# Down-projection of a gated FFN: four activation tiles per PSUM bank instead of two, half of the columns at a time

## The chip, the cores and the metric

One core of a Trainium2 chip runs the whole kernel. TensorE (PE) does the matmuls, with its weight loads as a row of their own (PEld); VectorE (DVE), ScalarE (ACT) and GpSimd (POOL) do the rest; SyncE (SP) issues the transfers. The metric is the device time of the program in microseconds (us), the median over several runs.

## The reference, cut to what matters

One decoder block over 2048 tokens of width 1024, in float32. A state-space branch and a sparse attention branch (an indexer picks 256 keys for each query) are merged by gates and added to the residual `x`; a SwiGLU feed-forward network of width 2816 follows:

```python
x = x + merged @ w_out
h2 = rms(x, norm2_g)
x = x + (silu(h2 @ w_ffn_gate) * (h2 @ w_ffn_up)) @ w_ffn_down
```

The change concerns the last product, `... @ w_ffn_down`, of shape (2048, 2816) by (2816, 1024).

## The kernel before, in words

**Float32 in three products.** Each operand is split into a high and a low part of a reduced float32 format, and `mm3` adds three matmuls (high by high, high by low, low by high) into one PSUM bank of 128 x 512 values. So one 128-row slice of a contraction costs three matmuls.

**Three generators and a planner.** The program is written as generators: the state-space branch, the attention branch, and the dense part (merge, output projection, FFN). A planner, the class `Pace`, runs them when the program is built, not on the chip: it keeps for each engine the time at which it would be free, adds a cost of its own for each instruction, and each time lets that generator go on whose next step can start (attention is asked before the dense part). What comes out is one fixed order of instructions for each engine; on the chip every engine works through its own in that order. All instructions are recorded by one helper, so the trace puts all of them on line L206. The steps of the attention's search for the 256 best keys (`search`) are counting passes on VectorE (tile `jkd`) and ScalarE (`jka`); one on VectorE may be placed while VectorE is, by the plan, at most `AHEAD` = 7 us further than PE. The cost of such a pass in the plan (a `tensor_scalar` with an accumulated output over 2-byte values) is

```python
RATE = {"DVE": (1.05e-3, 0.07), ...}      # us per element, us each
cost = size * r + c
cost -= size * r / 2                      # all operands of 2 bytes
cost += 0.14                              # accum_out
```

**The dense part** works in four blocks of 512 tokens (`block`, `tb` = 0 to 3). A block computes the merge (tiles `act`, `mg`) and the output projection into the residual `x1` (tile `x` in the trace), normalizes and transposes it (tiles `h`), and then goes over the 22 slices `f` of the FFN's width. `up(f)` makes gate and up product of a slice (48 matmuls, tiles `ww` for weights and `f` for banks), and `gate` and `join` turn them into an activation tile `at` (high and low part, 128 x 512 each) on ScalarE and VectorE. After every second `up`, `down` multiplies the two activation tiles of the pair before with their two slices of `w_ffn_down` (tile `wd`): for four token tiles and two halves of the columns it sums 2 x 3 matmuls in a bank, and VectorE adds the bank to `x1`. The last pair is multiplied right after `up(21)`.

**Banks.** While the attention is not finished a block has three PSUM banks for this, and four more during the search; the last block has eight.

**Weights.** In block 0 each weight is loaded raw (512 KB), split into high and low by two instructions on any of three engines, and the pair is stored to DRAM (`wc`, 1 MB); later blocks load the pair from there. The class `Rings` keeps one list of items in the order of use; an item is only issued when all before it are. Tiles of the kind "w" have a ring of three. Tiles of the kind "d" hold two items each, and their ring holds one such tile (two in the last block): the next two items are issued or split after `drop("d")`, when the last matmul has read the tile. A block's last items stand ahead of the next block's first in the list. All transfers go through SP's queue in order. Between `up(21)` and the last `down`, SP also issues the loads of the next block's `act` tiles (`load_branch`, 4 MB).

Of the kernel before, what the change touches and what calls it, by code (L numbers as in the profile page):

```python
# [13 lines left out]
F32R = mybir.dt.float32r  # L14
# [20 lines left out]
NF = DFF // 128  # L35
# [16 lines left out]
class Pace:  # L52
# [95 lines left out]
    def at(self, eng, *what):  # L148

        return lambda: self.when(eng, what) + (None,)  # L150
# [215 lines left out]
class Block:  # L366
# [1257 lines left out]
    def weights(self):  # L1624

        a = self.a
        items = []
        for ct in range(KD):
            items.append(("w", lambda raw, ct=ct: [
                (raw[:, i * 512:(i + 1) * 512].rearrange("p (k c) -> p k c", k=4),  # L1630
                 a[w][0, :, ct * 128:(ct + 1) * 128].rearrange("(k p) c -> p k c", p=128))
                for i, w in enumerate(("w_proj_ssm", "w_proj_attn"))]))
        for cg in range(4):
            for b in range(2):
                items.append(("w", lambda raw, cg=cg, b=b: [
                    (raw.rearrange("p (k c) -> p k c", k=4),
                     a["w_out"][0, b * 512:(b + 1) * 512, cg * 256:(cg + 1) * 256]
                     .rearrange("(k p) c -> p k c", p=128))]))
        for f in range(NF):
            for w in ("w_ffn_gate", "w_ffn_up"):  # L1640
                items.append(("w", lambda raw, f=f, w=w: [
                    (raw.rearrange("p (k c) -> p k c", k=KD),
                     a[w][0, :, f * 128:(f + 1) * 128].rearrange("(k p) c -> p k c", p=128))]))

            n = f if f % 2 == 0 else f + 1 if f == NF - 1 else 0
            for q in range(max(n - 2, 0), n):
                items.append(("d", lambda raw, q=q: [(raw, a["w_ffn_down"][0, q * 128:(q + 1) * 128])]))
        copies = [self.dram.tile([128, 2, 1024], F32, name=f"wc{i}") for i in range(len(items))]
        return [(kind, parts, copy, tb > 0) for tb in range(NB) for (kind, parts), copy in zip(items, copies)]

    def load_branch(self, bigp, br, tb):

        z = bigp.tile([128, 2, 4, TB], F32R, name=f"act{br}")
        for k in range(4):
            self.nc.sync.dma_start(z[:, :, k].bitcast(F32), (self.act_d, self.att_d)[br][tb][:, :, k])
        return z

    def block(self, tb, bigp, ld, nps, nd):

        nc, a, at = self.nc, self.a, self.pace.at  # L1660
        n = TB
        t0 = tb * TB
        nt = n // 128
# [3 lines left out]
        with ExitStack() as st:  # L1667
# [25 lines left out]
            def ready(*w):  # L1693
                return at("PE", free, *w)

            with ExitStack() as sm:
                mp = self.pool(sm, "mg", 1)
                mg = mp.tile([128, 2, KD, n], F32R, name="mg")
                with ExitStack() as sp:
# [16 lines left out]
                    for q, (ct, br) in enumerate([(0, 0), (1, 0), (0, 1), (1, 1)] +  # L1716
                                                 [(ct, br) for ct in range(2, KD) for br in range(2)]):
                        w = ld.get("w", 1 if q == 1 else 0)
                        w = w.rearrange("p z a (b k c) -> p (z a) b k c", b=2, k=4)[:, :, br]
# [16 lines left out]
                        if q in (4, 6, 8, 10):  # L1736
                            t = q // 2 - 2
# [25 lines left out]
                for cg in range(D // NC):  # L1763
                    cl = slice(cg * NC, (cg + 1) * NC)
                    for t in range(0, nt, 2):
                        for k in range(KD):
                            if k % 2 == 0:

                                late = t == nt - 2 and k >= 4
                                w = ld.get("w", 0 if late or k < 4 else 1)  # L1770
                                w = w.rearrange("p z a (k c) -> p (z a) k c", k=4)
# [3 lines left out]
                            for j in range(2):  # L1775
                                tl = slice((t + j) * 128, (t + j + 1) * 128)
# [17 lines left out]
                def up0(g, between=()):  # L1794

                    first[g] = bank(False)
                    sl = slice(g * 256, (g + 1) * 256)
                    for i in range(2):
                        w = ld.get("w", i).rearrange("p z a (k c) -> p (z a) k c", k=KD)
                        for k in range(KD):  # L1800
                            if k % 4 == 0:
                                yield at("PE", w)
                            z = hT[k // 4]
                            self.mm3(first[g][:, i * 256:(i + 1) * 256], w[:, 0, k], w[:, 1, k], z[:, 0, k % 4, sl],
                                     z[:, 1, k % 4, sl], i == k == 0, i == 1 and k == KD - 1)
                            if k % 2 == 1:
                                ld.tick()
                        if i == 0:
                            for t in between:
                                yield ready(hs[t])  # L1810
                                turn(t)
# [8 lines left out]
                yield ready(*hT)  # L1820
                yield from up0(0, (2, 3))
                self.pace.tight = False
            ap = self.pool(st, "fa", 3)
            tp = self.pool(st, "ft", 2)
            ld.ring("d", self.pool(st, "fd", nd), nd, 2)

            def gate(p):

                t = tp.tile([128, p.shape[1]], F32, name="t", tag="t")
                if self.exps:  # L1830

                    nc.scalar.activation(t, p, AF.Tanh, scale=0.5)
                    nc.vector.scalar_tensor_tensor(t, t, 1.0, p, op0=ALU.add, op1=ALU.mult)
                    return t, 0.5
                nc.scalar.activation(t, p, AF.Silu)
                return t, 1.0

            def join(t, c, p, hi, lo):
                nc.vector.scalar_tensor_tensor(t, t, c, p, op0=ALU.mult, op1=ALU.mult)
                self.split(t, hi, lo, nc.scalar, nc.vector)  # L1840

            def up(f, acts):
                if f == 0:
                    yield ready(*hT)
                    yield from up0(1)
                    for _ in range(2):
                        ld.drop("w")
                    for g, p in enumerate(first):
                        sl = slice(g * 256, (g + 1) * 256)
                        t, c = gate(p[:, :256])  # L1850
                        join(t, c, p[:, 256:], acts[:, 0, sl], acts[:, 1, sl])
                    return
                for i in range(2):
                    w = ld.get("w").rearrange("p z a (k c) -> p (z a) k c", k=KD)
                    yield ready(w, *hT)
                    p = bank()
                    for k in range(KD):
                        z = hT[k // 4]
                        self.mm3(p, w[:, 0, k], w[:, 1, k], z[:, 0, k % 4], z[:, 1, k % 4], k == 0, k == KD - 1)
                        if k == KD - 1:  # L1860
                            ld.drop("w")
                        if k % 2 == 1:
                            ld.tick()
                            if k < KD - 1:
                                yield at("PE")
                    if i == 0:
                        t, c = gate(p)
                join(t, c, p, acts[:, 0], acts[:, 1])

            def out(t):  # L1870
                nc.sync.dma_start(self.out[0, t0 + t * 128:t0 + (t + 1) * 128], x1[:, t])

            def down(acts, last):
                w = ld.get("d")
                for t in range(nt):
                    tl = slice(t * 128, (t + 1) * 128)
                    for cg in range(2):
                        cl = slice(cg * 512, (cg + 1) * 512)
                        yield ready(w, *acts)
                        p = bank()  # L1880
                        for f in range(2):
                            self.mm3(p, acts[f][:, 0, tl], acts[f][:, 1, tl], w[:, 0, f, cl], w[:, 1, f, cl],
                                     f == 0, f == 1)
                        if t == nt - 1 and cg == 1:
                            ld.drop("d")
                        ld.tick()
                        nc.vector.tensor_tensor(x1[:, t, cl], p, x1[:, t, cl], op=ALU.add)
                    if last and t > 0:
                        out(t - 1)
                if last:  # L1890
                    out(nt - 1)

            prev = None
            for c in range(NF // 2):
                acts = []
                for f in (2 * c, 2 * c + 1):
                    acts.append(ap.tile([128, 2, n], F32R, name="at"))
                    yield from up(f, acts[-1])
                    if f % 2 == 0 and prev:
                        yield from down(prev, False)  # L1900
                prev = acts
            if tb + 1 < NB:
                self.act = [self.load_branch(bigp, br, tb + 1) for br in range(1 + (self.attended >= 4 * (tb + 2)))]
            yield from down(prev, True)
            more.close()
            self.lent = False
            del ld.pools["d"]
# [78 lines left out]
```

## Time and profile before

| | |
|---|---|
| median of 3 runs | 3467.05 us (3461.62 to 3470.55) |
| the profiled execution: its own time | 3462.75 us |
| its span, first to last instruction | 3460.6 us |
| mean granted TensorE clock | 0.965 |
| busy: PE / VectorE / ScalarE / GpSimd | 93% / 62% / 36% / 20% |

Read as stretches (us from the span's start): up to about 1044 projections, state-space branch and first attention tiles; block 0 from there to 1685, block 1 to 2342, block 2 to 2996, block 3 to the end. The search for the key tiles 8 to 11 lies in about 1392 to 1800, that for 12 to 15 in about 2088 to 2450; attention proper in 1827 to 2088 and 2523 to 2900.

### The profile page before, as it was taken

To read this page: it belongs to the slowest core of one execution; us is meant where nothing else is said; L and a number is where in the kernel's file an instruction comes from. 1 tells how busy PE (TensorE), PEld (TensorE's weight loads), DVE (VectorE), ACT (ScalarE), POOL (GpSimd) and SP (SyncE) were. 2 spreads that over 40 slices of the span, in tenths; PEclk is the share of its full clock that TensorE was granted. 3 is DMA by queue.
4 is the path that set the end of the run, shared out by engine and by line. 5 is a ranking of instruction groups with operands and counts; after the bars stand their busy time and mean duration, and the time that the engine had idled before them with its cause. 6 is when DMAs were issued, how large, how long until landed. Compare 5 with 4: busy or idle time off the path is not lost. (4 is left out here: it accounts for less than half of the span.)

```text
span 3460.6 us, 44348 instructions
## 1 busy us (share of the span) xinstructions
PE 3201.6 (93%) x16292; PEld 2698.5 (78%) x16292; DVE 2133.6 (62%) x4306; ACT 1261.8 (36%) x2187; POOL 706.1 (20%) x1003
## 2 busy tenths in 40 slices
PE   6999999898878999989889999988899999999999
PEld 5889777676756888767688888767788888798887
DVE  4565665656496666788776766996856664222222
ACT  3141444445542544465024444771233442010000
POOL 3333686852213122244100000001000000000000
PEclk8999999999988999999999999999999999999999
DMA  4834333433448566567755233556453324755544
GB/s 134 248 119 121 117 110 89 147 124 105 146 148 300 208 212 228 182 232 244 286 184 194 97 133 135 194 195 242 176 200 121 134 86 152 282 214 215 195 170 182
DMA packets 321529, 605.69 MB, mean 175 GB/s; under 512 B 52896, under 2 KB 205216, under 8 KB 290592
## 3 DMA queue, kind: packets, MB, share of 16 engines
q1 hardware_dynamic: 321312, 602.86, 49.9%
q8 instruction: 128, 2.10, 0.3%
q14 instruction: 89, 0.73, 0.1%
HBM read 434.71 MB, written 166.89 MB: 174 GB/s over the span
## 5 line engine op out<-in xcount | busy, mean ns | idle before, releaser
L206 PE MATMUL f<-h,ww 128*128 128x512 f32 (+1 forms) x4416 | 1012.8, 383 | 3.0 <-DVE h L206 1.4
L206 PEld LDWEIGHTS f<-h,ww 128*128 128x128 f32 x4416 | 800.6, 190 | 159.9 <-DVE h L206 2.2
L206 PE MATMUL f<-wd,at 128*128 128x512 f32 x2112 | 530.8, 403 | 60.4 <-ACT at L206 31.9
L206 PEld LDWEIGHTS f<-wd,at 128*128 128x128 f32 x2112 | 403.5, 194 | 156.3 <-ACT at L206 27.9
L206 PE MATMUL gps<-hT,gw 128*128 128x512 f32 x1536 | 390.5, 404 | 17.3 <-ACT gsg L206 14.7
L206 ACT ACTIVATE jka<-S,tr 128x1024 bf16<-128x1024 f32 (+6 forms) x217 | 305.6, 1408 | 172.4 <-DVE tr L206 127.0
L206 PEld LDWEIGHTS gps<-hT,gw 128*128 128x128 f32 x1536 | 287.9, 192 | 81.5 <-ACT gsg L206 17.3
L206 DVE TENSOR_TENSOR x<-f,x 128x512 f32<-128x512 f32 x352 | 237.2, 686 | 91.3 <-PE f L206 90.5
L206 PE MATMUL mm<-w,hT 128*128 128x512 f32 (+1 forms) x1152 | 282.2, 403 | 7.4 <-DVE hT L206 7.1
L206 DVE SCALAR_TENSOR_TENSOR t<-t,f 128x512 f32<-128x512 f32 (+1 forms) x124 | 82.3, 664 | 329.5 <-PE f L206 284.4
L206 PEld LDWEIGHTS mm<-w,hT 128*128 128x128 f32 x1152 | 242.3, 241 | 32.5 <-DVE hT L206 8.5
L206 DVE TENSOR_TENSOR tl<-pt,th 128x512 fp32r<-128x512 f32 (+1 forms) x288 | 183.9, 658 | 131.7 <-ACT th L206 130.4
L206 ACT CAST th<-pt 128x512 fp32r<-128x512 f32 (+1 forms) x288 | 156.0, 563 | 233.5 <-PE pt L206 231.5
L206 POOL TENSOR_TENSOR g<-g,g 128x512 f32<-128x512 f32 x32 | 42.1, 1317 | 915.9 <-issue 551.8
L206 PE MATMUL f<-act,ww 128*128 128x512 f32 x768 | 190.8, 410 | 29.2 <-DMA act<-act 9.0
L206 PE MATMUL f<-ww,mg 128*128 128x256 f32 x1536 | 197.6, 291 | 18.3 <-DMA ww<-wc 10.0
L206 PEld LDWEIGHTS f<-ww,mg 128*128 128x128 f32 x1536 | 193.8, 199 | 21.3 <-issue 8.5
L206 PEld LDWEIGHTS f<-act,ww 128*128 128x128 f32 x768 | 150.8, 199 | 69.0 <-issue 14.3
L206 ACT ACTIVATE P<-P,m 128x1024 f32<-128x1024 f32 (+7 forms) x192 | 172.1, 899 | 72.6 <-DVE m L206 72.0
L206 PE MATMUL lg<-kk,q 128*128 128x512 f32 (+1 forms) x640 | 184.1, 390 | 5.8 <-DMA kk<-kk 3.7
L206 ACT ACTIVATE t<-f 128x512 f32<-128x512 f32 (+1 forms) x92 | 53.0, 576 | 331.7 <-PE f L206 331.6
L206 ACT CAST at<-t 128x512 fp32r<-128x512 f32 (+1 forms) x92 | 55.2, 600 | 325.2 <-DVE t L206 325.1
(347 smaller groups left out, 4577.1 us busy)
## 6 DMA issues: line engine op xcount, KB each, us to landing
ww<-wc SPq DMA_DIRECT2D x180, 1024.0 KB, 5.0
wd<-wc SPq DMA_DIRECT2D x66, 1024.0 KB, 8.5
wc<-ww SPq DMA_DIRECT2D x60, 1024.0 KB, 7.8
raw<-in_w_in_dram SPq DMA_DIRECT2D x104, 256.0 KB, 3.3
wc<-wd SPq DMA_DIRECT2D x22, 1024.0 KB, 7.5
x<-in_x_dram SPq DMA_DIRECT2D x32, 512.0 KB, 5.2
gate<-gsg SPq DMA_DIRECT2D x64, 256.0 KB, 2.2
g<-gate SPq DMA_DIRECT2D x64, 256.0 KB, 5.3
```

The lines of the kernel that those rows point to most:

```text
L206: return f(*args, **kw)
```

## The change

Four activation tiles instead of two are summed in a bank, so that a bank takes 12 matmuls, and VectorE adds it to `x1` half as often. A call of `down` covers half of the columns (512) for four slices, in place of all columns for two; the items of `w_ffn_down` become 256 rows by 512 columns, still two to a tile. `due` says which quarter is multiplied after which `up`: slices q to q+3 have their first half after `up(q+4)` and their second after `up(q+6)`. Seven activation tiles are kept instead of three. Slices 0 to 19 make five groups of four; the second half of the fifth group and the pair 20, 21 (both halves, 6 matmuls to a bank) are multiplied after `up(21)`. The matmuls, their shapes and their number stay.

```diff
--- before.py
+++ after.py
@@ -1642,11 +1642,21 @@
                     (raw.rearrange("p (k c) -> p k c", k=KD),
                      a[w][0, :, f * 128:(f + 1) * 128].rearrange("(k p) c -> p k c", p=128))]))
 
-            n = f if f % 2 == 0 else f + 1 if f == NF - 1 else 0
-            for q in range(max(n - 2, 0), n):
-                items.append(("d", lambda raw, q=q: [(raw, a["w_ffn_down"][0, q * 128:(q + 1) * 128])]))
+            for q, cg in self.due(f):
+                for p in range(q, min(q + 4, NF), 2):
+                    items.append(("d", lambda raw, p=p, cg=cg: [
+                        (raw.rearrange("p (f c) -> p f c", f=2),
+                         a["w_ffn_down"][0, p * 128:(p + 2) * 128, cg * 512:(cg + 1) * 512]
+                         .rearrange("(f p) c -> p f c", p=128))]))
         copies = [self.dram.tile([128, 2, 1024], F32, name=f"wc{i}") for i in range(len(items))]
         return [(kind, parts, copy, tb > 0) for tb in range(NB) for (kind, parts), copy in zip(items, copies)]
+
+    def due(self, f):
+
+        full = NF // 4 * 4
+        if f == NF - 1:
+            return [(full - 4, 1)] + [(full, cg) for cg in range(2)]
+        return [(f - 4 - f % 4, f % 4 // 2)] if f >= 4 and f % 2 == 0 else []
 
     def load_branch(self, bigp, br, tb):
 
@@ -1820,7 +1830,7 @@
                 yield ready(*hT)
                 yield from up0(0, (2, 3))
                 self.pace.tight = False
-            ap = self.pool(st, "fa", 3)
+            ap = self.pool(st, "fa", 7)
             tp = self.pool(st, "ft", 2)
             ld.ring("d", self.pool(st, "fd", nd), nd, 2)
 
@@ -1870,38 +1880,43 @@
             def out(t):
                 nc.sync.dma_start(self.out[0, t0 + t * 128:t0 + (t + 1) * 128], x1[:, t])
 
-            def down(acts, last):
-                w = ld.get("d")
+            def down(q, cgs):
+
+                w = ld.get("d").rearrange("p z a (f c) -> p z (a f) c", f=2)
+                nf = min(4, NF - q)
                 for t in range(nt):
                     tl = slice(t * 128, (t + 1) * 128)
-                    for cg in range(2):
+                    for cg in cgs:
                         cl = slice(cg * 512, (cg + 1) * 512)
-                        yield ready(w, *acts)
+                        yield ready(w, *(acts[q + f] for f in range(nf)))
                         p = bank()
-                        for f in range(2):
-                            self.mm3(p, acts[f][:, 0, tl], acts[f][:, 1, tl], w[:, 0, f, cl], w[:, 1, f, cl],
-                                     f == 0, f == 1)
-                        if t == nt - 1 and cg == 1:
+                        for f in range(nf):
+                            z, o = acts[q + f], f + nf * (cg if len(cgs) > 1 else 0)
+                            self.mm3(p, z[:, 0, tl], z[:, 1, tl], w[:, 0, o, cl0], w[:, 1, o, cl0],
+                                     f == 0, f == nf - 1)
+                            if f % 2 == 1:
+                                ld.tick()
+                                if f < nf - 1:
+                                    yield at("PE")
+                        if t == nt - 1 and cg == cgs[-1]:
                             ld.drop("d")
-                        ld.tick()
                         nc.vector.tensor_tensor(x1[:, t, cl], p, x1[:, t, cl], op=ALU.add)
-                    if last and t > 0:
+                    if len(cgs) > 1 and t > 0:
                         out(t - 1)
-                if last:
+                if len(cgs) > 1:
                     out(nt - 1)
 
-            prev = None
-            for c in range(NF // 2):
-                acts = []
-                for f in (2 * c, 2 * c + 1):
-                    acts.append(ap.tile([128, 2, n], F32R, name="at"))
-                    yield from up(f, acts[-1])
-                    if f % 2 == 0 and prev:
-                        yield from down(prev, False)
-                prev = acts
+            acts, cl0 = {}, slice(0, 512)
+            for f in range(NF):
+                acts[f] = ap.tile([128, 2, n], F32R, name="at")
+                yield from up(f, acts[f])
+                if f < NF - 1:
+                    for q, cg in self.due(f):
+                        yield from down(q, (cg,))
             if tb + 1 < NB:
                 self.act = [self.load_branch(bigp, br, tb + 1) for br in range(1 + (self.attended >= 4 * (tb + 2)))]
-            yield from down(prev, True)
+            yield from down(NF // 4 * 4 - 4, (1,))
+            yield from down(NF // 4 * 4, (0, 1))
             more.close()
             self.lent = False
             del ld.pools["d"]
```

## Rows read from the trace of the kernel before

**Rows 1.** page, part 1 (busy time by engine) and part 2 (40 slices)

```profile
PE 3201.6 (93%) x16292; PEld 2698.5 (78%) x16292; DVE 2133.6 (62%) x4306; ACT 1261.8 (36%) x2187; POOL 706.1 (20%) x1003
...
PE   6999999898878999989889999988899999999999
```

**Rows 2.** page, part 5, costliest groups: busy us, mean ns | idle before, releaser

```profile
L206 PE MATMUL f<-wd,at 128*128 128x512 f32 x2112 | 530.8, 403 | 60.4 <-ACT at L206 31.9
...
L206 DVE TENSOR_TENSOR x<-f,x 128x512 f32<-128x512 f32 x352 | 237.2, 686 | 91.3 <-PE f L206 90.5
```

**Rows 3.** windows: stretch, its length, busy us (instructions) per engine, clock, DMA

```profile
1465.00:1655.00 190.00, 166.77 (x671) 133.04 (x670) 169.10 (x308) 105.86 (x137) 88.20 (x41) 0.93 0.69 236
1655.00:1690.00 35.00, 18.70 (x70) 14.46 (x69) 33.27 (x63) 0.62 (x1) 0.00 (x0) 0.76 0.64 248
...
2175.00:2315.00 140.00, 130.68 (x556) 105.46 (x555) 129.69 (x268) 108.39 (x114) 0.00 (x0) 0.98 0.46 176
2315.00:2342.00 27.00, 13.47 (x50) 10.19 (x48) 25.66 (x52) 14.48 (x16) 0.00 (x0) 0.76 0.70 249
...
2523.00:2983.00 460.00, 460.00 (x2501) 390.33 (x2500) 265.02 (x552) 164.80 (x305) 0.00 (x0) 1.00 0.38 143
```

**Rows 4.** windows of tile x alone, the additions to the residual: VectorE is third

```profile
1465.00:1655.00 190.00, 0.00 (x0) 0.00 (x0) 25.88 (x39) 0.00 (x0) 0.93 0.69 236
...
2175.00:2315.00 140.00, 0.00 (x0) 0.00 (x0) 20.67 (x32) 0.00 (x0) 0.98 0.46 176
```

**Rows 5.** waits of PE, 1465 to 1655: total, times, longest us

```profile
PE f L206 <- DVE wd L206: 9.4, 4, 2.6
PE f L206 <- DVE un L206: 6.9, 3, 3.5
```

**Rows 6.** timeline of PE, block 3: start, us, instructions [idle before, releaser]

```profile
3422.06 11.04 PE L206 MATMUL f<-wd,at 128*128 128x512 f32 x48
3432.94 11.04 PE L206 MATMUL f<-h,ww 128*128 128x512 f32 x48
...
3445.48 10.77 PE L206 MATMUL f<-wd,at 128*128 128x512 f32 x45 [0.82 <-ACT at L206]
```

**Rows 7.** groups of VectorE by form: counting passes of the search

```profile
L206 DVE TENSOR_SCALAR_CACHE_REDUCE jkd<-H,tf 128x1664 bf16<-128x1664 uint16 x16 | 31.1, 1941 | 0.2
...
L206 DVE TENSOR_SCALAR_CACHE_REDUCE jkd<-H,tf 128x1280 bf16<-128x1280 uint16 x16 | 24.7, 1542 | 0.4
```

**Rows 8.** timeline of PE, end of block 0

```profile
1671.48 13.28 PE L206 MATMUL f<-wd,at 128*128 128x512 f32 x45 [15.52 <-ACT at L206]
1685.55 27.79 PE L206 MATMUL f<-act,ww 128*128 128x512 f32 x120 [0.78 <-DVE x L206]
```

**Rows 9.** timeline of VectorE, end of block 0

```profile
1670.09 0.69 DVE L206 SCALAR_TENSOR_TENSOR t<-t,f 128x512 f32<-128x512 f32 x1
```

**Rows 10.** timeline of PE, end of block 1

```profile
2324.86 12.63 PE L206 MATMUL f<-wd,at 128*128 128x512 f32 x45 [9.05 <-ACT at L206]
2341.97 28.22 PE L206 MATMUL f<-act,ww 128*128 128x512 f32 x114 [4.48 <-DVE x L206]
```

**Rows 11.** timeline of PE, end of block 2

```profile
2985.10 10.74 PE L206 MATMUL f<-wd,at 128*128 128x512 f32 x45 [0.82 <-ACT at L206]
```

**Rows 12.** tile wd: its conversions (ns min/median/max) and its loads

```profile
L206 ACT CAST wd<-raw x12: 1037/1046/1062, 1202.4 to 1645.4; 128x1024 fp32r<-128x1024 f32 x12
...
L206 POOL TENSOR_TENSOR wd<-raw,wd x6: 2390/2400/2928, 1260.2 to 1647.9; 128x1024 fp32r<-128x1024 f32 x6
...
DMA to landing us min/median/max: 5.2/8.2/10.8
```

**Rows 13.** windows of 4 us, end of block 1, columns as in rows 3

```profile
2320.00:2324.00 4.00, 0.00 (x0) 0.00 (x0) 3.90 (x9) 3.22 (x4) 0.00 (x0) 0.50 0.98 291
```

**Rows 14.** DMA issues: engine, op, count, KB each, median us to landing

```profile
raw<-in_w_ffn_down_dram SPq DMA_DIRECT2D x22, 512.0 KB, 4.4
...
raw<-in_w_out_dram SPq DMA_DIRECT2D x8, 512.0 KB, 6.1
```

## The prediction

> **What bounds the kernel now.** I read the page first: PE is busy for 93% of the span, VectorE for 62%, and most of PE's slices show a 9 [rows 1]. So PE bounds the kernel, and a change that leaves its matmuls alone can only win back time in which PE stands still or runs slowly. The page's groups then say what the change touches: 2112 matmuls of the down-projection, before which PE was idle for 60.4 us in all, and 352 additions of 686 ns, 237.2 us of VectorE [rows 2]. The third view, the windows, shows where the idle time lies. While attention proper runs, 2523 to 2983, PE is busy for 460.00 of 460 us: there, fewer additions buy nothing. During the two searches VectorE is busy for 169.10 of 190 us and 129.69 of 140 us, while PE is not full [rows 3].
>
> How much PE loses there needs its pace. In the last block, where nothing disturbs it, 48 matmuls take 3432.94 - 3422.06 = 10.88 us, 0.2267 us each [rows 6]. At that pace the 671 matmuls of 1465 to 1655 need 152.1 us, so 37.9 us are lost; the 556 of 2175 to 2315 need 126.0, so 14.0 are lost [rows 3] (an estimate, since some matmuls are narrower, and the loss then larger). What PE waits for there is VectorE: in the first stretch 9.4 us for the split of a weight tile and 6.9 us where VectorE's last instruction was one of the search (`un`) [rows 5], which I read as a bank whose addition stood in the queue behind the search.
>
> The fourth view is the timeline at the ends of the blocks. After `up(21)` the last pair needs the activation tile that has just been made. Block 0: PE waits 15.52 us, because `join` only comes up on VectorE at 1670.09, behind counting passes [rows 8, 9]. Block 1: 9.05 us, and 4.48 us at the next block's start for the last additions [rows 10]. Blocks 2 and 3: 0.82 us each [rows 6, 11].
>
> **The change part by part.** All sums are against the profiled execution's 3462.75 us, which is 4.3 below the median of the runs.
>
> *Additions.* A block has 5 x 8 + 8 = 48 instead of 88, so 160 of 352 go: 160 x 0.686 = 110 us of VectorE. Outside the searches PE is full or VectorE is mostly idle, and this costs and gives nothing. Inside them 39 and 32 additions take 25.88 and 20.67 us [rows 4]; half of that, 12.9 + 10.3 = 23.2 us, leaves VectorE. The upper bound of the gain is therefore 23, if VectorE alone sets the pace there. The lower bound is 0, for this reason: the planner puts counting passes into VectorE's plan until that is 7 us ahead of PE. Time that the additions free in the plan is filled with passes, and the plan prices these too low: by its formula a pass over 1280 values is 0.672 + 0.07 + 0.14 = 0.88 us and one over 1664 is 1.08, where the trace has 1.54 and 1.94 [rows 7]. What PE loses in a search is then mainly this mispricing, some 0.66 and 0.86 us a pass, however few additions there are. Against that stands that a bank now takes 12 matmuls, so that with the same banks PE can run twice as long ahead of a late VectorE. I take 10.
>
> *Order at the end of a block.* After `up(21)` PE now has the second half of the fifth group, 48 matmuls or 10.9 us, before it needs the newest tile. This hides 0.82 us in blocks 2 and 3 and up to 10.9 in blocks 0 and 1.
>
> *What is late next: the last weight tile.* In blocks 0 to 2 the ring "d" holds one tile. Before, the last one was fetched during `up(21)`. Now its predecessor is in use until the 48 matmuls are done, and only then is the last one loaded or split, with PE behind it and, in a search or with the attention finished, nothing else to do. Queued behind it on SP are the next block's first "w" items; 48 matmuls of 10.9 us in the last `down` cover them. The next block's `act` loads are issued ahead, at the end of `up(21)`, and have one `down` more to land than before.
>
> - Block 0: split at need. The high part takes 1.05 us on ScalarE, the low part 2.40 on GpSimd [rows 12]; for two items, partly in a row, I take 5. Bounds: 3.4, and 15 if the low part goes to VectorE's queue behind the search, as `join` did.
> - Blocks 1 and 2: loaded at need. Such a load landed after 5.2 to 10.8 us, 8.2 in the median [rows 12]; with little else on the queues by then I take 7.
> - A wait costs more than itself. After 9.05 us of idle, 45 matmuls took 12.63 us, against 10.74 after 0.82 us [rows 10, 11]: 1.9 us. The granted clock was 0.50 in 2320 to 2324, the lower level of 1.2 GHz, after PE had stopped at about 2316 [rows 13]. The Trainium skill, TensorE: Matmul & The Clock Gate, section "HAM oscillation — how this bites in real kernels", says that an array which waits for its next operand slice starts its next matmuls at the low clock; it speaks against a new wait of this kind, and the row agrees.
>
> So for the ends of the blocks. Block 0 loses now 15.52 + 2.5 (13.28 against 10.74) + 0.78 = 18.8; afterwards 5, 1.5 of slow clock and, since VectorE is still late, some 4 for the last additions, as at the end of block 1: 10.5. Gain 8 (bounds -3 and 15). Block 1 loses 9.05 + 1.9 + 4.48 = 15.4; afterwards 7 + 1.9 + 4.5 = 13.4. Gain 2 (bounds -2 and 10). Block 2 loses 0.82 and afterwards 7 + 1.9: a loss of 8 (bounds 4.4 and 12). Block 3 has a ring of two: gain 0.8.
>
> *Smaller edits.* The raw loads of `w_ffn_down` fall into runs of 2 KB instead of 4 KB. The nearest rows are its own 4.4 us to landing and 6.1 for `w_out`, in runs of 1 KB [rows 14]: at worst 1.7 us later, hidden by the two `up` (22 us) in which they are fetched; 0. Seven activation tiles take 16 KB more of each partition; a tile is written again only seven slices later, after both its readers: 0. A step between the halves of a bank lets the planner go elsewhere after 6 matmuls, as before: 0.
>
> Sum: 10 + 8 + 2 - 8 + 0.8 = 13 faster. 3462.75 - 13 = 3450; in terms of the median 3467.05 - 13 = 3454.
>
> **The rivals.**
>
> *VectorE sets the pace of the searches.* For it: 89% and 93% busy, and PE's waits there are for VectorE. Against it: the planner's filling, above. Then the full 23 is won, and since VectorE comes out of the search earlier, the waits at the ends of blocks 0 and 1 shrink too, say by another 5: 23 + 8 + 2 + 5 - 7 = 31 faster, 3436.
>
> *Slower: the one-deep ring of down tiles.* The place is the last `down` of blocks 0 to 2. If the last split of block 0 queues behind the search (15 + 2.5 + 4.5 instead of 18.8: 3 lost), and the loads of blocks 1 and 2 take the longest landing, 10.8 + 1.9 (2 and 12 lost), that is 17 slower; it decides as soon as the searches give back less than 7. For it: in block 2 the wait has nothing before it to replace. Against it: 6 to 8 us is the commoner landing. With nothing won in the searches, 3484. The Trainium skill, Trainium Kernel Development and Optimization, section "Best Practices", asks for double buffers so that transfers overlap with compute, which here would be a second tile in this ring; the loads that now land unseen behind `up(21)` agree with it.
>
> *No change.* The planner refills the searches (0 instead of 10) and the rest stands: 3 faster, 3464.
>
> **How the numbers follow.** This kernel's measurement can tell about 0.3%, 10.4 us, from no change: faster means below 3456.6, slower above 3477.4. The forecast (4 to 24 faster, that is 3443 to 3463 for the median) has a chance of 0.42, of which 0.28 lie beyond 10.4 us and 0.14 within. The full relief has 0.20, all faster. No change has 0.22, of which 0.20 within and 0.02 slower, with the ends of the blocks a little worse than summed. The one-deep ring has 0.16, slower. Together 0.48, 0.34 and 0.18. The bounds of the terms added up would reach from 45 faster to 17 slower; the range goes from 37 faster (beyond the full relief's 31) to 11 slower, part of the way to the ring's case: 3430 to 3478.
>
> **What would show it.** In the trace after: 192 additions; VectorE still about 90% busy in the searches, in fewer microseconds if the relief is real; no wait for `at` after `up(21)`; in its place, 48 matmuls later, PE waiting some 5 us for `wd` in block 0 and some 7 us for the load `wd<-wc` in blocks 1 and 2. The prediction is wrong if these waits are far longer, if the searches lose as much as before (refill) or almost nothing (relief), or if the planner's other order opens waits elsewhere.

## The result and the profile after

The change takes 3493.35 us (median of 4 runs, 3484.99 to 3497.03) against 3467.89 before: a ratio of 1.0073 [1.005, 1.0096]. It is 25 us slower, where 13 us faster had been forecast, and lies outside the range. The profiled execution took 3497.03 us, its span is 3495.1 us; the difference of the two spans, 34.5 us, is what the traces explain, and some 9 us of it come from which runs were profiled: the one after lies 3.7 us above its median, the one before 5.1 below its own.

The costliest groups after, which answer to [rows 2]:

```profile
L206 PE MATMUL f<-wd,at 128*128 128x512 f32 x2112 | 529.2, 406 | 86.9 <-DVE wd L206 20.5 <-DVE un L206 19.9 <-ACT at L206 15.2
...
L206 DVE TENSOR_TENSOR x<-f,x 128x512 f32<-128x512 f32 x192 | 130.9, 688 | 138.9 <-PE f L206 138.6
```

VectorE has 160 additions less and does 106 us less of them, as said. Yet PE's idle time before the down-projection rose from 60.4 to 86.9 us. The windows view, cut at the first `act` matmul of each block, says where (columns as in [rows 3]):

```profile
0.00:1713.30 1713.30, 1495.44 (x7325) 1245.35 (x7325) 1145.70 (x2415) 718.91 (x1302) 659.58 (x961) 0.94 0.52 169
1713.30:2382.80 669.50, 626.58 (x3269) 532.32 (x3269) 494.28 (x965) 315.98 (x474) 14.68 (x16) 0.96 0.46 168
2382.80:3035.00 652.20, 636.33 (x3460) 543.17 (x3461) 316.63 (x625) 187.94 (x344) 13.47 (x12) 0.98 0.46 169
3035.00:3495.10 460.10, 453.89 (x2241) 385.42 (x2240) 96.61 (x143) 40.87 (x70) 13.46 (x12) 1.00 0.54 202
```

Before, block 0 ended at 1685.5 and the next three took 656.5, 653.7 and 464.9 us. So 27.8 and 13.0 us are lost up to the ends of blocks 0 and 1, which hold the searches, and 1.5 and 4.8 are won in blocks 2 and 3.

**The search in VectorE's queue.** Windows of the counting passes alone (tile `jkd`; the third column is VectorE's busy time and their number). Each fence has the search for tiles 8 to 11 ahead of block 0's end and behind it, then that for 12 to 15 around block 1's end. First the kernel before, then the change:

```profile
1392.00:1685.50 293.50, 84.45 (x111) 0.92 0.64 224
1685.50:1830.00 144.50, 25.70 (x34) 0.96 0.65 240
2080.00:2342.00 262.00, 105.67 (x104) 0.96 0.48 174
2342.00:2500.00 158.00, 40.88 (x40) 0.92 0.59 214
```

```profile
1392.00:1713.30 321.30, 106.84 (x140) 0.90 0.61 214
1713.30:1850.00 136.70, 2.97 (x4) 0.94 0.60 218
2080.00:2382.80 302.80, 142.51 (x140) 0.95 0.45 170
2382.80:2550.00 167.20, 4.03 (x4) 0.94 0.58 208
```

The passes are the same, 144 in each search (one that lies across the cut at 1685.5 is counted twice); their place is not. Ahead of block 0's end there are now 140 instead of 111, ahead of block 1's 140 instead of 104. That is 22 and 37 us of VectorE, in front of the work that the block still needs of it; the prediction had counted 23 us of additions freed in both searches.

**Inside the search.** PE's waits from 1465 to 1655, which answer to [rows 5]:

```profile
PE f L206 <- DVE wd L206: 20.5, 5, 6.4
PE f L206 <- DVE un L206: 17.5, 3, 7.4
```

These 38.0 us are all that PE waits in this stretch; before it was 23.3 (the 16.3 of [rows 5], 5.7 for `at` and 1.3 for `x`). The timelines of PE and VectorE, side by side, show the first two of the eight waits:

```profile
1486.17 0.39 PE L206 MATMUL f<-wd,at 128*128 128x512 f32 x1
1493.93 2.93 PE L206 MATMUL f<-wd,at 128*128 128x512 f32 x6 [7.37 <-DVE un L206]
1502.02 12.30 PE L206 MATMUL f<-wd,at 128*128 128x512 f32 x41 [5.17 <-DVE wd L206]
```

```profile
1491.32 1.41 DVE L206 TENSOR_SCALAR_CACHE_REDUCE jkd<-H,tr 128x1152 bf16<-128x1152 bf16 x1
...
1492.65 1.22 DVE L206 TENSOR_TENSOR wd<-raw,wd 128x1024 fp32r<-128x1024 f32 x1
...
1499.06 2.91 DVE L206 TENSOR_TENSOR wd<-raw,wd 128x1024 fp32r<-128x1024 f32 x1
```

The low part of a `wd` tile is split on VectorE. The first split stands directly behind counting passes; it ends at 1492.65 + 1.22 = 1493.87 and PE goes on at 1493.93. The second stands behind one more pass, `join` and 1.60 us in which VectorE waits for ScalarE; it ends at 1501.97, and PE goes on at 1502.02. The other six waits end with a split in the same way. The releaser `un` in the first row is the next instruction on VectorE, not the cause.

In the kernel before, `un` mostly stood for something else. PE and VectorE there:

```profile
1482.18 2.45 PE L206 MATMUL f<-wd,at 128*128 128x512 f32 x6 [3.48 <-DVE un L206]
```

```profile
1481.44 0.69 DVE L206 TENSOR_TENSOR x<-f,x 128x512 f32<-128x512 f32 x1
```

The addition ends at 1481.44 + 0.69 = 1482.13 and PE goes on at 1482.18. The wait of 1.23 us at 1522.04 ends with an addition too, and only the third, 2.18 us at 1590.70, with a split. So 4.7 of the 6.9 us were additions stuck behind the search, as the prediction had read them. In the change these waits are gone, and those for the splits are longer.

**The ends of the blocks.** PE at the end of block 0, which answers to [rows 8]:

```profile
1675.09 0.79 PE L206 MATMUL f<-wd,at 128*128 128x512 f32 x1 [8.14 <-ACT wd L206]
1677.53 6.16 PE L206 MATMUL f<-wd,at 128*128 128x512 f32 x17 [1.65 <-POOL wd L206]
...
1699.13 2.93 PE L206 MATMUL f<-wd,at 128*128 128x512 f32 x6 [3.80 <-DVE x L206]
1713.28 16.96 PE L206 MATMUL f<-act,ww 128*128 128x512 f32 x61 [11.21 <-DVE x L206]
```

The timelines of VectorE and of ScalarE there (the first row answers to [rows 9]):

```profile
1672.76 0.68 DVE L206 SCALAR_TENSOR_TENSOR t<-t,f 128x512 f32<-128x512 f32 x1
...
1700.81 3.36 DVE L206 TENSOR_TENSOR_SCAN S<-ones,fin 128x1536 f32<-128x1536 f32 x1
...
1712.54 2.48 DVE L206 TENSOR_TENSOR x<-f,x 128x512 f32<-128x512 f32 x4
```

```profile
1673.47 0.62 ACT L206 CAST at<-t 128x512 fp32r<-128x512 f32 x1 [22.21 <-DVE t L206]
1674.00 1.99 ACT L206 CAST wd<-raw 128x1024 fp32r<-128x1024 f32 x2
```

At this place the wait for `at` is gone, but `join` itself comes up on VectorE even later (1672.76, before 1670.09). The high part of the last `wd` tile stands on ScalarE behind `join`'s cast, which had waited 22.21 us for VectorE, so the late search is paid once more under another name. The block's last additions then stand behind the search's final stage (the scan at 1700.81), and the next block's first matmul waits 11.21 us for them. From 1392 to the end of block 0 PE's waits in the dense part add up to 68.8 us, against 39.6 before, which covers the 27.8 us. PE at the ends of blocks 1 and 2, which answer to [rows 10, 11]:

```profile
2358.93 9.71 PE L206 MATMUL f<-wd,at 128*128 128x512 f32 x30 [6.34 <-DMA wd<-wc]
...
2382.80 12.44 PE L206 MATMUL f<-act,ww 128*128 128x512 f32 x42 [7.25 <-DVE x L206]
...
3021.76 13.45 PE L206 MATMUL f<-wd,at 128*128 128x512 f32 x48 [5.53 <-DMA wd<-wc]
```

These are the loads at need that the prediction had named, 6.34 and 5.53 us, with the slower matmuls behind them (13.45 for 48, against 10.88 undisturbed). The wait for `at` is not gone from block 1: it has moved forward, to 9.57 us at 2246 and 5.59 at 2320.

### The profile page after: what moved, and what is told of

It is laid out like the page before. It is cut to its first block, busy times and chain, and to the rows that moved or that the text cites. A ratio compares the mean times of both kernels' runs of the same rounds, so it can differ in the third digit from the quotient of the medians.

```text
span 3495.1 us, 44164 instructions
## 1 busy us (share of the span) xinstructions
PE 3212.2 (92%) x16292; PEld 2706.2 (77%) x16292; DVE 2053.2 (59%) x4147; ACT 1263.7 (36%) x2189; POOL 701.2 (20%) x1001
## 5 line engine op out<-in xcount | busy, mean ns | idle before, releaser
L206 PE MATMUL f<-wd,at 128*128 128x512 f32 x2112 | 529.2, 406 | 86.9 <-DVE wd L206 20.5
L206 DVE TENSOR_TENSOR x<-f,x 128x512 f32<-128x512 f32 x192 | 130.9, 688 | 138.9 <-PE f L206 138.6
```

Source lines behind the costliest of these rows:

```text
L206: return f(*args, **kw)
```

## The experiments

Two theories. **The refilled plan:** the planner fills the VectorE time that the saved additions free with counting passes that it prices too low, so that VectorE comes later than before to all that PE needs of it. **The late tile:** the one-deep ring makes the last pair's weights late, and that is the loss. No kernel leaves out or changes any of the computation. Differences between kernels are given in microseconds of the ratios, for which the kernel before was run again each time; the medians alone give up to 4 us more or less for a kernel.

**1. The change, with the plan charged for the additions that are gone.** The program on the chip has 192 additions; only the planner's clock still counts the time of the others.

```diff
 nc.vector.tensor_tensor(x1[:, t, cl], p, x1[:, t, cl], op=ALU.add)
+if nf == 4:
+    self.pace.free["DVE"] += 512 * 1.05e-3 + 0.07
```

> The changed kernel with one line more: after each addition of a bank with four slices the planner's clock of VectorE is put forward by the cost of the addition that was saved (0.61 us), so that it places the search's passes about as densely as before. The instructions are those of the change. Theory 1 (the planner fills the freed time with passes that it prices too low, so VectorE runs later and PE waits for it): most of the 41 us that blocks 0 and 1 lost comes back, some 10 stay at the ends of blocks 1 and 2: 3460 to 3477. Theory 2 (the new wait for the last down tile at the end of blocks 0 to 2 is the loss): nothing changes, 3485 to 3500.

Measured: 3452.71 us, ratio 0.9965 [0.9956, 0.9975]. This is 0.0108, or 37 us, below the change, with the late tile still there (it waits 7.39 us for the load at the end of block 1). The passes, in the view and stretches used above:

```profile
1392.00:1680.37 288.37, 83.84 (x112) 0.92 0.65 235
...
2080.00:2326.64 246.64, 109.67 (x108) 0.96 0.50 186
```

They are back at 112 and 108. The refilled plan holds, and more came back than its range had allowed for.

**2. The kernel before, with the plan freed of half of its additions.** All 352 additions stay on the chip.

```diff
 nc.vector.tensor_tensor(x1[:, t, cl], p, x1[:, t, cl], op=ALU.add)
+self.pace.free["DVE"] -= (512 * 1.05e-3 + 0.07) / 2
```

> The kernel before, all its additions kept, with the planner's clock of VectorE put back by half the cost of an addition (0.30 us) after each. Theory 1: the search's passes move forward under the FFN of blocks 0 and 1 and PE waits more, as in the change or worse, since the additions are still there: 3480 to 3510. Theory 2: no down tile is late, so no difference: 3460 to 3475.

Measured: 3492.2 us, ratio 1.0078 [1.0061, 1.0095], the loss of the whole change, made by the plan alone, with 129 and 138 passes ahead of the blocks' ends. That it is as large as the change's is chance: here the additions are still carried out.

**3. and 4. A corrected price for a pass, in both kernels.** Without the halving, the plan's 1280 values cost 1.55 us and 1664 cost 1.96, where the trace has 1.54 and 1.94 [rows 7].

```diff
-elif eng == "DVE" and op in ("tensor_scalar", "tensor_tensor") and short:
+elif eng == "DVE" and op in ("tensor_scalar", "tensor_tensor") and short and "accum_out" not in kw:
     cost -= size * r / 2
```

The change:

> The changed kernel, with the planner's price of a counting pass corrected: the halving for 2-byte operands is not applied where the instruction has an accumulated output (1.55 instead of 0.88 us for 1280 values; the trace has 1.54). Theory 1: VectorE no longer falls behind the plan, the waits for wd, at and x within blocks 0 and 1 mostly go, and of the waits at the ends of the blocks those for VectorE: 3420 to 3460. Theory 2: the waits for the last down tile stay, and the rest is as before: 3475 to 3500.

The kernel before:

> The kernel before with the corrected price of a counting pass. Theory 1: what PE lost in the two searches (some 52 us there and more at the ends of blocks 0 and 1) came from the price, and most of it comes back: 3415 to 3445. If the price does not matter in the kernel before, 3455 to 3475. Beside e4_after_priced it shows what the change is worth under a plan that is right: a few us, since block 2 then still pays for the late down tile.

Measured: 3415.92 us, 0.9863 [0.9849, 0.9878] for the change, and 3419.38 us, 0.9864 [0.984, 0.9888] for the kernel before. One line of the planner is worth 47 us to either, and under the right price the change as it stands is worth nothing. The priced change came out 4 us below its range.

**5. and 6. Two activation tiles per bank in the new order**, so with 352 additions again; half of the columns, seven tiles and the ring stay. Unpriced and with the corrected price.

```diff
-                        p = bank()
                         for f in range(nf):
+                            if f % 2 == 0:
+                                if f:
+                                    yield ready(w)
+                                p = bank()
...
-                                     f == 0, f == nf - 1)
+                                     f % 2 == 0, f % 2 == 1)
...
-                                    yield at("PE")
+                                    nc.vector.tensor_tensor(x1[:, t, cl], p, x1[:, t, cl], op=ALU.add)
```

> The changed kernel with its sums of four undone: order, tiles and seven activation tiles as in the change, but each bank sums two slices and VectorE adds twice as often, as before (352 additions). Theory 1 (the planner's filling): the additions are back in the plan and so the passes go back to where they were, and the kernel is faster than the change although VectorE has 110 us more to do: 3455 to 3478. If VectorE's work itself set the pace: slower than the change, 3495 to 3520.

> The same (two slices per bank, 352 additions) with the corrected price of a counting pass. Beside e4_after_priced it shows what the 160 additions are worth when the plan is right. Theory 1: little, since the search then only takes longer under work that fills PE: 3412 to 3430. If the additions set the pace of the searches: 20 to 30 more than e4_after_priced, 3436 to 3446.

Measured: 3483.75 us, 1.0053 [1.0033, 1.0072], and 3415.86 us, 0.9844 [0.9814, 0.9874]. The first fell into neither range: giving the additions back wins only some 7 us of the 25. By itself this does not tell a second loss from a plan that is still too full in block 0 (131 passes, 111 before); experiment 7 does. The second cannot be told from the priced change: with the price right, 160 additions are worth nothing that shows.

**7. and 8. The last pair's weights through the ring of `w` tiles** (three deep), columns outermost in the last `down`. Unpriced and with the corrected price.

```diff
-items.append(("d", lambda raw, p=p, cg=cg: [
+items.append(("w" if q == NF // 4 * 4 else "d", lambda raw, p=p, cg=cg: [
...
-w = ld.get("d").rearrange("p z a (f c) -> p z (a f) c", f=2)
+kind = "w" if len(cgs) > 1 else "d"
+for cg in cgs:
+    w = ld.get(kind).rearrange("p z a (f c) -> p z (a f) c", f=2)
```

> The changed kernel, but the weights of the last pair of slices go through the ring of three w tiles, so that they are fetched during up(21) and the 48 matmuls after it; the last down takes one half of the columns after the other. Theory 2: the waits of 9.8, 6.3 and 5.5 us for the last down tile go, with the slow matmuls behind them, and all or nearly all of the loss: 3460 to 3475. Theory 1: only block 2's 5.5 us and its slow matmuls are won in full; in blocks 0 and 1 PE waits for VectorE's last additions instead: 3480 to 3490.

> The changed kernel with the corrected price and the last pair's weights in the ring of w tiles. In the trace of e4_after_priced PE waits 5.0 us for the split and twice 5.5 us for the load of the last down tile; these go, with the slow matmuls behind them: 3398 to 3412, 4 to 18 below e4_after_priced. If VectorE's last additions take the place of these waits: within 5 of it.

Measured: 3472.91 us, 1.0018 [1.0007, 1.0029], 19 us below the change, though 138 and 138 passes still stand ahead of the blocks' ends; and 3400.52 us, 0.9808 [0.9785, 0.9832], 19 below the priced change and the fastest of all kernels here. The first time lies in the range given for the late tile, which so is the second loss. But the plan is still full, and in this kernel the wait for `at` is back, behind the 48 matmuls that were to cover it: 3.83 us at the end of block 0, and at the end of block 1

```profile
2336.00 13.26 PE L206 MATMUL f<-ww,at 128*128 128x512 f32 x45 [9.23 <-ACT at L206]
```

In the kernel before it was 9.05 there [rows 10].

PE's timeline of the `w` ring with the corrected price at the end of block 1 is what the prediction had hoped for, with no wait:

```profile
2269.78 11.04 PE L206 MATMUL f<-wd,at 128*128 128x512 f32 x48
2280.66 11.04 PE L206 MATMUL f<-ww,at 128*128 128x512 f32 x48
2291.54 3.34 PE L206 MATMUL f<-act,ww 128*128 128x512 f32 x14
```

At the end of block 0 PE still waits 8.72 us for `at`, behind the same 48 matmuls.

This kernel is also 19 us faster than the kernel before under the same price (0.9808 against 0.9864, the intervals apart). So with both losses mended the change does win. Where the 19 us come from was not tried. By the traces it is not the end of block 0, which comes 10 us later; blocks 1 to 3 are 9, 13 and 11 us shorter, and PE in the priced kernel before waits 4.8 us for the attention's output (`act<-att`) at the start of block 3, where this one does not wait for it.

**9. Both corrections of the change: `w` ring and charged plan** (the edits of 1 and 7).

> The change with both corrections: the last pair's weights through the ring of w tiles, and the plan's VectorE charged 0.61 us after each addition of a sum of four, so that it has as much addition time as before. Taken alone, the first made the change 20 us faster and the second 41. If the refilled plan and the late last tile are two separate losses, they add up: 3493 - 41 - 20 = 3432, 3427 to 3442. If they are one loss (the late tile only hurts because VectorE is late, or the w ring only helps because its other order moves the plan), it stays at the better of the two, 3447 to 3457. The corrected pass price with the w ring took 3400.5; this one should stay above that, since the passes themselves are still priced too low.

Measured: 3438.12 us, 0.9931 [0.9916, 0.9946]. The ring gives 12 us on top of the charge, the charge 30 on top of the ring: two losses that nearly add up.

**10. The order alone: `w` ring and two tiles per bank** (the edits of 5 and 7), price uncorrected.

> What is left of the change when neither the plan is freed of additions (two tiles to a sum, 352 additions as before) nor the last pair's tile is late (ring of w tiles); price of a pass uncorrected. Left are only the order of the products (half of the columns at a time, a later start, 48 matmuls after the last up before the newest tile is needed). If refill and late tile are the whole loss, this is no slower than before: 3455 to 3468, by the two steps measured alone 3493 - 10 - 20 = 3463. If the order itself loses time in the searches (another loss beside the two), it stays above: 3475 to 3490.

Measured: 3467.07 us, 1.0015 [1.0004, 1.0026]: 5 us above the kernel before, 3 by the medians. With neither loss left, the new order wins nothing under the uncorrected price. PE's waits in it from 1392 to 1720:

```profile
PE f L206 <- DVE un L206: 19.8, 6, 6.4
PE f L206 <- DVE x L206: 7.2, 7, 1.9
PE f L206 <- DVE t L206: 6.7, 1, 6.7
PE f L206 <- DVE wd L206: 6.1, 3, 3.9
PE f L206 <- DMA ww<-wc: 5.0, 3, 2.6
```

The same view of the kernel before:

```profile
PE f L206 <- ACT at L206: 21.2, 4, 15.5
PE f L206 <- DVE wd L206: 9.4, 4, 2.6
PE f L206 <- DVE un L206: 6.9, 3, 3.5
PE f L206 <- DVE x L206: 2.1, 4, 0.9
```

The 5.0 us for loads lie behind the end of block 0. Without them it is 39.8 us against 39.6: the 21.2 for `at` are gone, and the other waits for VectorE have grown by as much. By the spans block 0 ends 2.3 us earlier than before and block 1 is 0.9 shorter; blocks 2 and 3 are 5.3 and 1.0 longer. In block 2 PE waits 15.3 us for the norm of the merge (`ss`, on VectorE), before 3.9, with 48 passes behind the end of block 1 in place of 40.

All kernels together, by the passes ahead of the ends of blocks 0 and 1 (from the windows, counted from 1392 and 2080) and the start of block 1's merge:

| kernel | ratio | passes | block 0 ends, us |
|---|---|---|---|
| the change | 1.0073 | 140, 140 | 1713.3 |
| `w` ring | 1.0018 | 138, 138 | 1695.3 |
| two per bank | 1.0053 | 131, 112 | 1700.4 |
| before, plan credited | 1.0078 | 129, 138 | 1705.6 |
| plan charged | 0.9965 | 112, 108 | 1680.4 |
| change, priced | 0.9863 | 112, 86 | 1671.4 |
| before | 1 | 111, 104 | 1685.6 |
| `w` ring, two per bank | 1.0015 | 109, 96 | 1683.2 |
| `w` ring, priced | 0.9808 | 98, 66 | 1666.6 |
| `w` ring, plan charged | 0.9931 | 92, 78 | 1661.6 |
| two per bank, priced | 0.9844 | 85, 68 | 1664.9 |
| before, priced | 0.9864 | 75, 50 | 1656.4 |

From the last row to the first, block 0 ends 0.88 us later for each pass that is placed ahead of it ((1713.3 - 1656.4) / 65), somewhat more than the 0.76 us that a pass takes (106.84 / 140). This is rough, since the kernels differ in more than their passes.

## Why the prediction was wrong, by its own steps

**What bounds the kernel: right.** PE bounds it on the whole, and in the searches PE waits for VectorE. Of the 6.9 us under `un` it read 4.7 rightly as additions. But in the change all eight waits from 1465 to 1655 end with a split of `wd`: what was won at the banks was lost again at the splits.

**Additions: the count and price right, the gain wrong.** The term was 10 faster, with bounds of 0 and 23. Step by step from two to four tiles per bank it measured 7 slower with the late tile (1.0053 to 1.0073) and 1 slower without (1.0015 to 1.0018), both within what these intervals can tell from nothing. Behind this nothing stand two large steps. Taking the additions out while the plan still counts their time makes the kernel 30 us faster (two per bank against plan charged, 1.0053 to 0.9965; with the `w` ring 1.0015 to 0.9931, 29). Freeing the plan as well takes 37 and 30 back (0.9965 to 1.0073, 0.9931 to 1.0018). The first step is not the additions alone, since the plans differ: with plan charged 19 passes fewer stand ahead of block 0's end (112 against 131), with the `w` ring 17 (92 against 109), at 0.76 us some 14 and 13 us of VectorE. What the additions are worth under one and the same plan no run shows. The step that failed here is the lower bound. The prediction named the refill and the mispricing, yet took from them only that the gain may be 0. It stopped short of the next thought: 0.66 us too little for each pass means that every pass drawn forward makes VectorE later, so a refill costs. Experiment 2 shows it without the change: 27 us slower.

**Order at the end of a block: this step failed most.** It counted block 0's 18.8 us and block 1's 15.4 us of loss as savings that 48 matmuls would buy, less what the late tile costs: gains of 8 and 2. Experiment 10 has the 48 matmuls and no late tile, and is 5 us slower than before, where this step by itself would have made it some 27 faster (18.8 - 4, 15.4 - 4.5, and 0.8 twice). Blocks 0 and 1 won 2.3 and 0.9 of the 14.8 and 10.9. The wait for `at` was not a cost of the order. It was the place at which PE's lead over a late VectorE ran out. Cover it, and PE runs out at the next bank, split, join or norm; with the plan full, it runs out at `at` once more (9.23 us in experiment 7). With a shorter queue on VectorE, under the corrected price, the end of block 1 has no wait at all (experiment 8); that of block 0 keeps its wait for `at`, and why is open.

**The last weight tile: right in mechanism, and in size but for block 0.** Predicted were 5, 7 and 7 us; the trace has 9.8 (8.14 + 1.65), 6.34 and 5.53. (The 8.2 us to landing of [rows 12] counts stores along with the loads; the loads alone have a median of 8.5.) Block 0's excess is the split's place on ScalarE behind `join`'s cast, the case that the upper bound of 15 stood for, on another engine. By the runs the tile is worth 19 (the change), 13 (two per bank, 1.0053 to 1.0015), 12 (plan charged) and 19 us (priced), each give or take 6 to 10. The `w` ring also leaves fewer passes ahead of block 0's end (138, 109, 92, 98 against 140, 131, 112, 112). So a wait for the tile in the plan seems to draw passes forward too; that is argued from these counts and was not measured by itself.

**Block 2: the loss came, and was covered.** 5.53 us of wait and 2.6 of slower matmuls make 8.1, predicted were 8.9. But the 36 passes that had moved into block 1 no longer lay here, and the block came out 1.5 us shorter. **Block 3:** 0.8 predicted, 4.8 measured: the 0.82 before the last `down` is gone, and so are 2.79 us within block 3's merge, where the kernel before had waited for a load.

**The smaller edits** cost nothing that shows. **The rivals:** full relief named the right pace-setter and the wrong sign; the one-deep ring, 17 slower at 0.16, was nearest to what came (25), in number only: its late loads came, but the larger loss, the refill, is not in it. The sum forgot that its two big gains, searches and block ends, were claims on the same VectorE time.

## What to carry to other kernels

In a program whose order is planned ahead, work taken off an engine is refilled by the plan at the plan's prices: compare these prices with the trace's durations first, since a pass priced at half makes relief in the plan into lateness on the chip (here one corrected price was worth 47 us, and the change nothing until the price and the late tile were both mended, then 19). A long wait at the end of a stage in which one engine is late all along is not a saving to be had there; add up all of PE's waits that this engine causes, whatever their names, and ask what makes its queue shorter. A reordering that puts the last weights behind a one-deep ring needs a second place for them in the same edit.

## What the runs showed of the hardware

VectorE's smallest instructions are held up by GpSimd. Timelines of VectorE and of GpSimd in the change:

```profile
1464.24 1.81 DVE L206 SCALAR_TENSOR_TENSOR tr<-un,tr 128x2 int32<-128x2 int32 x1
...
1472.70 1.78 DVE L206 SCALAR_TENSOR_TENSOR tr<-un,tr 128x1 int32<-128x1 int32 x1
...
1478.49 0.16 DVE L206 SCALAR_TENSOR_TENSOR tr<-un,tr 128x1 int32<-128x1 int32 x1
...
1674.73 1.54 DVE L206 TENSOR_SCALAR_CACHE_REDUCE jkd<-H,tf 128x1280 bf16<-128x1280 uint16 x1
```

```profile
1464.14 1.89 POOL L206 TENSOR_TENSOR ww<-raw,zeros 128x1024 fp32r<-128x1024 f32 x1
...
1472.07 2.40 POOL L206 TENSOR_TENSOR ww<-raw,ww 128x1024 fp32r<-128x1024 f32 x1
...
1675.12 4.68 POOL L206 TENSOR_TENSOR wd<-raw,wd 128x1024 fp32r<-128x1024 f32 x2 [23.95 <-ACT wd L206]
```

An update of one or two values that takes 0.16 us alone took 1.81 and 1.78, and ended at 1466.05 and 1474.48, with GpSimd's instructions (1466.03 and 1474.47). The counting pass at 1674.73, with a GpSimd split beside it from 1675.12 on, took its usual 1.54. The 2.91 us of the `wd` split at 1499.06 (usually 1.22) overlap a GpSimd instruction (1498.50 to 1500.89) in the same way. The Trainium skill, SBUF — State Buffer, section "Who interferes with whom", states that VectorE and GpSimd share a pair of ports as an exclusive lock, taken by a VectorE instruction with two SBUF inputs against a GpSimd instruction that reads SBUF, and not by a `tensor_scalar` that also writes its accumulator. The trace agrees on both. The group of these updates in the change:

```profile
L206 DVE SCALAR_TENSOR_TENSOR tr<-un,tr 128x1 int32<-128x1 int32 x232 | 72.5, 312 | 8.0
```

At 312 ns in the mean instead of 160 they cost VectorE 232 x 0.152 = 35 us more over the kernel, an estimate that puts all of the excess down to GpSimd. In the kernel before the mean is 337, so this is not what the change made slower. How much of VectorE's lateness this makes beside the price of the passes was not tried. GpSimd's splits lie in block 0 alone, so they may be why that block still ends late under the corrected price.
